# Second SwiGLU product: part loads a round ahead, residual tiles loaded singly, the final norm's halves on two engines

## The chip, the cores and the metric

One core of a Trainium2 chip runs the whole program. The metric is the device time of one launch in microseconds. The program before was timed three times.

## The reference, cut to what matters

The program is one layer of a streaming encoder on 1024 tokens of width 1024, in float32. After three token mixers and an output projection with a residual, which give `x`, comes the part that is changed:

```python
h = rms_norm(x, norm_ffn_g[l])
gate, up = jnp.split(h @ w_ffn_in[l], 2, axis=-1)
x = x + (jax.nn.silu(gate) * up) @ w_ffn_out[l]
...
return rms_norm(x, final_norm_g)   # x * rsqrt(mean(x*x) + 1e-6) * g
```

The hidden width of the SwiGLU is 2816, which is 22 tiles of 128, or 11 pairs of tiles ("j").

## The kernel before, in words

Every float32 product is made of three float32r matmuls (lines 132 to 134) on operands split into a high part (cast on ACT, line 125) and a low part (subtraction on DVE, line 126). The large products follow a Strassen-like scheme: a block product is seven products (p = 0 to 6) of sums of quarters instead of eight. The sums of the left side are made on DVE (line 901).

The class `Blocks` runs such products over units n. `make` prepares the left operand of the next product, up to seven products ahead. `product` issues the matmuls of (n, p). `after` empties or adds what they gave. For each n the sums "a" and "b" stand in one PSUM tile of two banks, and "c" in a third bank, begun by a copy of "a" on ACT (line 958).

The gate and up products are `fb`, over 22 units. Each finished quarter of silu(gate) times up is written to the DRAM tensor `m_d` by line 1231, from tiles of the pool `fb`. Meanwhile `right_units` splits the weights of the second product and parks them in the DRAM tensor `wt_d`.

The second product is `f2`, of class `Second`, over 16 rounds. A round (t, j0, j1) takes token tiles t and t + 4 and the pairs j0 to j1 of the hidden width; rounds 0 and 1 take two pairs, so 6 matmuls for a product, and later ones two or three pairs. Its left side is read back from `m_d` in two halves (i = 0, 1) by line 1318, inside `mid_sums`: one half in the two buffers "wr", which the weights of `fb` use before, the other in two buffers "mr" of the pool `fc`; round 0 has both halves in "wr". Its right side are tiles `tt` in a ring of 14, read from `wt_d` by line 1296; tiles 12 and 13 of the ring lie in `fc`. Each product of a round is added to the residual tile `x3` at line 1334; `load_x3(t)` (lines 1298 to 1302) brings tokens t and t + 4 as two transfers into one tile of the pool `keep`. Tiles wait for each other as wholes: a product into "a" waits until the addition that reads "b" of the same round is done.

The pool `fc` is opened at line 1382, after `fb` is released, and takes the same memory.

In the last round of a token tile `final(t, half)` makes the norm: ACT squares a half with a sum (line 1398), a small DVE operation follows (line 1400), and with the second half come another small DVE operation (1403), a power of -0.5 on POOL (1404) and on DVE two products of x, the root and the gain `fng` (1406), each with a DMA to the output (1407).

All DMAs here are issued by SP, which takes them in order. The order on every engine comes from a planner that simulates the program: of the instructions that are ready in its simulation it takes the one that stands first in the program, so that instructions can be moved ahead of blocked ones. On the chip each engine then keeps that order.

Of the kernel before, what the change touches and what calls it, by code (L numbers as in the profile page):

```python
# [7 lines left out]
F32 = mybir.dt.float32  # L8
F32R = mybir.dt.float32r
U8 = mybir.dt.uint8  # L10
AF = mybir.ActivationFunctionType
ALU = mybir.AluOpType
# [4 lines left out]
P = 128  # L17
S = 1024
D = 1024
# [9 lines left out]
EPS = 1e-6  # L29
# [42 lines left out]
def body(nc, tc, I, out):  # L72
    x_d, w_d, wf_d, wfup_d, par_d, lq_d, cst_d, msk_d, ffg_d, fng_d = I
    vec, act, pe, pool, sp = nc.vector, nc.scalar, nc.tensor, nc.gpsimd, nc.sync
# [3 lines left out]
    wp = tc.alloc_tile_pool(name="wp", bufs=2)  # L78
# [6 lines left out]
    y2 = lambda name: yp.tile([P, HALF], F32, tag="y2", name=name)  # L85
    s2 = lambda name: sp4.tile([P, HALF], F32, tag="s2", name=name, bufs=4)
# [5 lines left out]
    sm = cpool.tile([P, 32], F32, name="sm")  # L92
# [25 lines left out]
    def f(ap):  # L118
        return ap.bitcast(F32)
# [30 lines left out]
    def like(ap, src):  # L150
        if len(src.shape) == 2:
            return ap
        return ap[:, 0:src.shape[1] * src.shape[2]].rearrange("p (k n) -> p k n", k=src.shape[1])
# [6 lines left out]
    def operand(src, pin=False):  # L160
        if not spare:
            th, tl = wtiles()
            spare.extend((th[:, i, :], tl[:, i, :]) for i in range(2))
        wh, wl = spare.popleft()
        hilo(like(wh, src), like(wl, src), src, pin)
        return wh, wl
# [71 lines left out]
    def spawn(gen, after=0):  # L238
        clock["seq"] += 1
        heapq.heappush(events, (clock["now"] + after, clock["seq"], gen))  # L240
# [47 lines left out]
    def drain():  # L288
        while events:
            clock["now"] = max(clock["now"], events[0][0])  # L290
            resume()
# [47 lines left out]
    def hs(half):  # L339
        return slice(half * HALF, (half + 1) * HALF)  # L340
# [81 lines left out]
    for j in range(2):  # L422
        vec.tensor_tensor(out=lt[:, j * 64:(j + 1) * 64], in0=lq[:, j * 128:j * 128 + 64],
                          in1=lq[:, j * 128 + 64:j * 128 + 128], op=ALU.mult)
# [470 lines left out]
    def lefts(alloc, a11, a21, a12, a22):  # L895
        s_ = {0: a11, 3: a12, 5: a22}
        p = None

        def comb(to, a, b, op):
            s_[to] = like(alloc("s"), a11)  # L900
            vec.tensor_tensor(out=s_[to], in0=a, in1=b, op=op)

        while True:
            p = yield operand(s_[p]) if p is not None else None
            if p == 1:
                comb(1, a21, a22, ALU.add)
            elif p == 2:
                comb(2, s_[1], a11, ALU.subtract)
            elif p == 4:
                comb(4, a11, a21, ALU.subtract)  # L910
            elif p == 6:
                comb(6, a12, s_[2], ALU.subtract)

    def of(blocks):
        return lambda n, p: [tuple(b[:, k, :] for b in blocks[right[p]]) for k in range(4)]
# [105 lines left out]
    order = [(0, 0), (0, 3), (0, 1), (0, 2), (0, 4)]  # L1021
# [185 lines left out]
    order = [(0, 0), (0, 3), (1, 0), (1, 3), (0, 1), (1, 1), (0, 2), (1, 2), (0, 4), (1, 4), (0, 6), (1, 6), (0, 5)]  # L1207
# [34 lines left out]
    def t4_block():  # L1242
        for k in range(4):
            u, v = c2("u"), c2("v")
            for o, p in ((u, 0), (v, 1)):
                vec.tensor_tensor(out=o, in0=f(B["21"][p][:, k, :]), in1=f(B["T2"][p][:, k, :]), op=ALU.subtract)
            vec.tensor_tensor(out=u, in0=u, in1=v, op=ALU.add)
            hilo(B["T4"][0][:, k, :], B["T4"][1][:, k, :], u)
            yield 3
# [37 lines left out]
    tt, x3 = {}, {}  # L1287

    def load_t(i):
        if i >= NTL:  # L1290
            return
        at = i % RING
        pool_, tag = (keep, "kb") if at in (0, 1, 6, 7) else (big, "big") if at < 12 else (fcs["fc"], "tt")
        tt[i] = pool_.tile([P, 4, HALF], F32R, tag=tag, name="tt", bufs=8 if at < 12 else 2)
        n = 2 if i == NTL - 1 and 7 * PAIRS % 2 else 4
        sp.dma_start(f(tt[i][:, 0:n, :]), wt_d[i][:, 0:n, :])

    def load_x3(t):
        x = keep.tile([P, 2, D], F32, tag="kb", name="x3")
        for i in range(2):  # L1300
            sp.dma_start(x[:, i, :], x2_d[t + 4 * i])
            x3[t + 4 * i] = x[:, i, :]


    ROUNDS = [(0, 0, 2), (1, 0, 2), (2, 0, 3), (3, 0, 3), (0, 2, 4), (1, 2, 5), (2, 3, 6), (3, 3, 6),
              (0, 4, 7), (1, 5, 8), (2, 6, 9), (3, 6, 9), (0, 7, 11), (1, 8, 11), (2, 9, 11), (3, 9, 11)]
    fcs = {}

    def mid_sums(n):
        t, j0, j1 = ROUNDS[n]  # L1310
        v = []
        for i in range(2):
            if i and n:
                raw = fcs["fc"].tile([P, 1024], F32, tag="mr", name="mr", bufs=2)
            else:
                raw = wp.tile([P, 1024], F32, tag="wr", name="wr", bufs=2)
            raw = raw[:, 0:(j1 - j0) * 2 * P].rearrange("p (j b c) -> p j b c", j=j1 - j0, b=2)
            sp.dma_start(raw, m_d[j0:j1, t, :, 2 * i:2 * i + 2, :].rearrange("j p b c -> p j b c"))
            v += [raw[:, :, b, :] for b in range(2)]
        return lefts(s2, *v)  # L1320

    def unit_of(j, p):
        u = 7 * j + p
# [25 lines left out]
    for i, at in last_use.items():  # L1349
        loads.setdefault(at, []).append(i + RING)  # L1350
    f2 = Second(order2, makes2, mid_sums, lambda n, p: [unit_of(j, p) for j in range(*ROUNDS[n][1:])],
                None, None, 0)

    fb = Blocks(order, makes, ffn_sums, of(B), finish, copy, 6)
    for _ in range(4):
        fb.make()
    for at, (n, p) in enumerate(order):
        if at == 4:
            drain()
            tail.release()  # L1360
            fbs.append(tc.alloc_tile_pool(name="fb", bufs=1))
            spawn(t4_block(), 7)
        for _ in range(2 if at > 4 else 1):
            if len(fb.made) < (4 if at < 12 else AHEAD):
                fb.make()
        fb.product(n, p)
        if at == 14:
            spawn(right_units(), 0)
        if n == NU - 1:
            for i in {0: (2, 3), 1: (4, 5), 2: (6, 7), 3: (8, 9), 6: (10, 11)}.get(p, ()):  # L1370
                load_t(i)
            for t in {4: (0, 1), 5: (2, 3)}.get(p, ()):
                load_x3(t)
        if fb.nxt == len(order) and f2.nxt < 7 and len(fb.made) + len(f2.made) < AHEAD:
            f2.make()
        fb.after(n, p)
# [4 lines left out]

    fc = tc.alloc_tile_pool(name="fc", bufs=1)
    fcs["fc"] = fc
    for i in (12, 13):
        load_t(i)
    fng = fc.tile([P, D], F32, tag="fng", name="fng")
    sp.dma_start(fng, fng_d)
    norm = {}

    def final(t, half):  # L1390

        if t not in norm:
            norm[t] = fc.tile([P, D], F32, tag="xn", name="xn", bufs=2)
            a, other = sm[:, t:t + 1], None
        else:
            a, other = sm[:, 8 + t:9 + t], sm[:, t:t + 1]
        xn = norm[t]
        act.activation(xn[:, hs(half)], x3[t][:, hs(half)], AF.Square, accum_out=a)
        if other is None:
            vec.tensor_scalar(out=a, in0=a, scalar1=D * EPS, scalar2=None, op0=ALU.add)  # L1400
            return
        rc = sm[:, 16 + t:17 + t]
        vec.tensor_scalar(out=rc, in0=a, scalar1=other, scalar2=1.0 / D, op0=ALU.add, op1=ALU.mult)
        pool.tensor_tensor(out=rc, in0=rc, in1=mhalf[:, 0:1], op=ALU.pow)
        for c in (hs(0), hs(1)):
            vec.scalar_tensor_tensor(out=xn[:, c], in0=x3[t][:, c], scalar=rc, in1=fng[:, c], op0=ALU.mult, op1=ALU.mult)
            sp.dma_start(out[t, :, c], xn[:, c])

    for at, (n, p) in enumerate(order2):
        for _ in range(2):  # L1410
            if len(f2.made) < AHEAD:
                f2.make()
        f2.product(n, p)
        f2.after(n, p)
        for i in loads.get(at, ()):
            load_t(i)
# [59 lines left out]
def _program(arrays):  # L1476
    import concourse.bacc as bacc

    nc = bacc.Bacc("TRN2", target_bir_lowering=False, num_devices=1, dynamic_dma_scratch_size=1024)
    ins = [nc.dram_tensor(n, v.shape, mybir.dt.from_np(v.dtype), kind="ExternalInput").ap() for n, v in arrays.items()]  # L1480
    out = nc.dram_tensor("out_0_dram", (NT, P, D), F32, kind="ExternalOutput").ap()
    with tile.TileContext(nc) as tc:
        body(nc, tc, ins, out)
    return nc
# [9 lines left out]
```

## Time and profile before

| | us |
|---|---|
| median of 3 runs | 2070.02 (2068.46 to 2072.39) |
| profiled execution, its own time | 2069.95 |
| its span in the profile | 2068.2 |
| PE busy | 2013.6 (97%) |
| DVE busy | 1466.8 (71%) |
| ACT busy | 924.8 (45%) |
| POOL busy | 56.7 (3%) |

The span is what the trace covers; 1.75 us of the execution's own time lie around it. "Idle before" in a row is the time in which the engine stood, and the arrow names what ended it. PEclk is the granted clock of the matmul engine as a share of its full 2.4 GHz; half of it, 1.2 GHz, is its other level. Sizes are in units of 128 partitions by elements.

### The profile page before, as it was taken

To read this page: it belongs to the slowest core of one execution; us is meant where nothing else is said; L and a number is where in the kernel's file an instruction comes from. 1 tells how busy PE (TensorE), PEld (TensorE's weight loads), DVE (VectorE), ACT (ScalarE), POOL (GpSimd) and SP (SyncE) were. 2 spreads that over 40 slices of the span, in tenths; PEclk is the share of its full clock that TensorE was granted. 3 is DMA by queue.
4 is the path that set the end of the run, shared out by engine and by line. 5 is a ranking of instruction groups with operands and counts; after the bars stand their busy time and mean duration, and the time that the engine had idled before them with its cause. 6 is when DMAs were issued, how large, how long until landed. Compare 5 with 4: busy or idle time off the path is not lost.

```text
span 2068.2 us, 27247 instructions
## 1 busy us (share of the span) xinstructions
PE 2013.6 (97%) x10280; PEld 1694.9 (82%) x10280; DVE 1466.8 (71%) x2314; ACT 924.8 (45%) x1960; POOL 56.7 (3%) x64
## 2 busy tenths in 40 slices
PE   7999999999999999999999999999999999969997
PEld 6888878799999888898988888878888878847775
DVE  7997878677667787877874475469776776446566
ACT  6434433445534455555555452235444445312223
POOL 1000000000000000000000000000000000000000
PEclk9999999999999999999999999999999999989999
DMA  4232243312324444425243644414676666776652
GB/s 157 97 127 88 82 130 104 117 47 67 98 73 116 134 112 100 97 65 133 68 108 108 227 162 140 137 67 140 227 250 223 234 236 230 254 289 237 229 184 87
DMA packets 125124, 298.75 MB, mean 144 GB/s; under 512 B 11744, under 2 KB 56416, under 8 KB 115264
## 3 DMA queue, kind: packets, MB, share of 16 engines
q1 hardware_dynamic: 122256, 290.19, 42.1%
q0 software_dynamic: 2736, 6.82, 2.1%
q8 instruction: 81, 1.33, 0.3%
q14 instruction: 51, 0.42, 0.1%
HBM read 183.19 MB, written 94.90 MB: 134 GB/s over the span
## 4 chain that ended last, share of the span: by engine, by line
PE 68%; issue 13%; DVE 9%; DMA 6%; ACT 3%; POOL 1%; SPq 0%; DVEq 0%; POOLq 0%; ACTq 0%
PE sc L132 11%; PE sc L133 11%; PE sc L134 11%; PE pb L132 11%; PE pb L133 11%; PE pb L134 10%; DVE acc L448 1%; DMA wr<-w_dram 1%; DMA m_d<-t 1%; DMA wo<-w_dram 1%; DVE wl L126 1%; DMA wt_d<-to 1%; PE pb L766 1%; ACT p L739 1%; POOL rs L139 1%
## 5 line engine op out<-in xcount | busy, mean ns | idle before, releaser
L448 DVE SCALAR_TENSOR_TENSOR acc<-up,par,acc 128x1024 f32<-128x1024 f32 x240 | 306.2, 1276 | 0.6
L132 PE MATMUL pb<-h,wh 128*128 128x512 f32 x704 | 281.0, 399 | 1.0 <-ACT hf L310 1.0
L134 PE MATMUL pb<-h,wl 128*128 128x512 f32 x704 | 275.5, 391 | 0.0
L133 PE MATMUL pb<-h,wh 128*128 128x512 f32 x704 | 275.3, 391 | 0.0
L125 ACT CAST wh<-wr 128x512 fp32r<-128x512 f32 (+2 forms) x265 | 157.2, 611 | 187.7 <-PE pb L133 68.6
L126 DVE TENSOR_TENSOR wl<-wr,wh 128x512 fp32r<-128x512 f32 (+2 forms) x265 | 176.2, 673 | 75.4 <-ACT wh L125 73.7
L125 ACT CAST wh<-s 128x512 fp32r<-128x512 f32 (+2 forms) x216 | 123.6, 580 | 216.7 <-PE sc L133 137.9
L134 PEld LDWEIGHTS pb<-h,wl 128*128 128x128 f32 x704 | 132.3, 188 | 28.4
L132 PEld LDWEIGHTS pb<-h,wh 128*128 128x128 f32 x704 | 132.7, 188 | 26.0 <-ACT hf L310 1.2
L133 PEld LDWEIGHTS pb<-h,wh 128*128 128x128 f32 x704 | 132.6, 188 | 23.6 <-issue 0.2
L132 PE MATMUL pb<-wh,h 128*128 128x256 f32 x512 | 148.4, 290 | 0.0
L126 DVE TENSOR_TENSOR wl<-s,wh 128x512 fp32r<-128x512 f32 (+2 forms) x216 | 134.8, 635 | 17.8 <-ACT wh L125 17.8
L134 PE MATMUL pb<-wh,h 128*128 128x256 f32 x512 | 144.8, 283 | 0.0
L133 PE MATMUL pb<-wl,h 128*128 128x256 f32 x512 | 144.7, 283 | 0.0
L132 PE MATMUL sc<-bT,wh 128*128 128x512 f32 x352 | 137.4, 391 | 0.9 <-DVE t L1223 0.8
L133 PE MATMUL sc<-bT,wh 128*128 128x512 f32 x352 | 137.0, 389 | 0.0
L134 PE MATMUL sc<-bT,wl 128*128 128x512 f32 x352 | 137.0, 389 | 0.0
L132 PE MATMUL sc<-tt,wh 128*128 128x512 f32 x264 | 107.7, 413 | 22.4 <-ACT wh L125 15.3
L133 PE MATMUL sc<-tt,wh 128*128 128x512 f32 x264 | 104.6, 396 | 0.0
L134 PE MATMUL sc<-tt,wl 128*128 128x512 f32 x264 | 104.1, 396 | 0.0
L1334 DVE TENSOR_TENSOR x<-x,sc 128x512 f32<-128x512 f32 x80 | 54.5, 685 | 67.8 <-PE sc L134 66.5
L132 PE MATMUL sc<-T,wh 128*128 128x512 f32 x256 | 100.0, 391 | 1.9 <-ACT c L986 1.4
(300 smaller groups left out, 4567.5 us busy)
## 6 DMA issues: line engine op xcount, KB each, us to landing
wr<-w_dram SPq DMA_DIRECT2D x146, 512.0 KB, 3.7
wt_d<-to SPq DMA_DIRECT2D x38, 1024.0 KB, 4.2
tt<-wt_d SPq DMA_DIRECT2D x38, 1024.0 KB, 5.6
m_d<-t SPq DMA_DIRECT2D x44, 256.0 KB, 4.2
wo<-w_dram SPq DMA_DIRECT2D x22, 512.0 KB, 5.8
k<-k SPq DMA_DIRECT2D x48, 128.0 KB, 2.6
kl<-kl SPq DMA_DIRECT2D x48, 128.0 KB, 2.4
xt<-x_dram SPq DMA_DIRECT2D x8, 512.0 KB, 8.1
```

The source lines that it names most:

```text
L125: a = act.copy(hi, src)
L126: b = vec.tensor_tensor(out=lo, in0=src, in1=f(hi), op=ALU.subtract)
L132: pe.matmul(o, ah, bh, start=start, stop=False, skip_group_check=more)
L133: pe.matmul(o, ah, bl, start=False, stop=False, skip_group_check=more)
L134: pe.matmul(o, al, bh, start=False, stop=stop, skip_group_check=more)
L139: pool.tensor_tensor(out=dst, in0=dst, in1=mhalf[:, 0:width], op=ALU.pow)
L448: op = vec.scalar_tensor_tensor(out=acc, in0=up[:, j:j + S], scalar=w, in1=acc, op0=ALU.mult, op1=ALU.add)
L739: act.activation((p0[:, 0:n], p1)[i], sc[i], AF.Exp, bias=st_[:, i:i + 1], accum_out=st_[:, 2 + i:3 + i])
L766: pe.matmul(ov[:, 0:P], parts[k // 4][:, c], a["v"][:, k, :], start=k == 0, stop=k == nk - 1)
L1334: vec.tensor_tensor(out=x, in0=x, in1=ch["bacaab"[p - 1]], op=ALU.add)
```

## The change: what it does

Part loads: `mid_sums` loads nothing of its own round any more. A new function `load_mid(n)` loads both halves of round n: round 0 into two small buffers "mr0" (tag "y2"), odd rounds into both "wr" buffers, even rounds from 2 on into both "mr" buffers of `fc`. Round 0 is asked for twelve products before the end of `fb`, round 1 once all left operands of `fb` are made, round 2 as the first thing in `fc`, and round n + 1 by `mid_sums(n)`.

Residual tiles: before, `load_x3(0)` to `load_x3(3)` (four times two transfers) stood in the last unit of `fb`. Now only `load_x3(0)` stands there, `load_x3(1)` after the opening of `fc` and the loads of round 2, and 2 and 3 with the first products of rounds 1 and 2. Ring tiles 12 and 13 and the gain `fng` move from the opening of `fc` to the first products of rounds 2 and 4.

Final norm: with the first half DVE now multiplies x by the gain; with the second half ACT scales that product by the root while DVE makes the other half as before. The gain is multiplied by 32 once, on ACT, so that the mean's division by 1024 falls away.

```diff
-    def mid_sums(n):
+    mid = {}
+
+    def load_mid(n):
+        if n >= len(ROUNDS) or n in mid:
+            return
         t, j0, j1 = ROUNDS[n]
-        v = []
+        mid[n] = []
         for i in range(2):
-            if i and n:
+            if n == 0:
+                raw = y2("mr0")
+            elif n % 2:
+                raw = wp.tile([P, 1024], F32, tag="wr", name="wr", bufs=2)
+            else:
                 raw = fcs["fc"].tile([P, 1024], F32, tag="mr", name="mr", bufs=2)
-            else:
-                raw = wp.tile([P, 1024], F32, tag="wr", name="wr", bufs=2)
...
+    def mid_sums(n):
+        if n:
+            load_mid(n + 1)
+        return lefts(s2, *mid[n])
...
-            for t in {4: (0, 1), 5: (2, 3)}.get(p, ()):
-                load_x3(t)
+            if p == 4:
+                load_x3(0)
+        if at == len(order) - 12:
+            load_mid(0)
+        if fb.nxt == len(order):
+            load_mid(1)
...
-    for i in (12, 13):
-        load_t(i)
+    load_mid(2)
+    load_x3(1)
     fng = fc.tile([P, D], F32, tag="fng", name="fng")
-    sp.dma_start(fng, fng_d)
...
+            act.activation(xn[:, c], x3[t][:, c], AF.Square, accum_out=sm[:, t:t + 1])
+            vec.tensor_tensor(out=xn[:, c], in0=x3[t][:, c], in1=fng[:, c], op=ALU.mult)
             return
...
+        vec.tensor_scalar(out=rc, in0=a, scalar1=sm[:, t:t + 1], scalar2=D * EPS, op0=ALU.add, op1=ALU.add)
         pool.tensor_tensor(out=rc, in0=rc, in1=mhalf[:, 0:1], op=ALU.pow)
-        for c in (hs(0), hs(1)):
-            vec.scalar_tensor_tensor(out=xn[:, c], in0=x3[t][:, c], scalar=rc, in1=fng[:, c], op0=ALU.mult, op1=ALU.mult)
-            sp.dma_start(out[t, :, c], xn[:, c])
+        o = hs(1 - half)
+        act.activation(xn[:, o], xn[:, o], AF.Copy, scale=rc)
+        vec.scalar_tensor_tensor(out=xn[:, c], in0=x3[t][:, c], scalar=rc, in1=fng[:, c], op0=ALU.mult, op1=ALU.mult)
+        for q in (o, c):
+            sp.dma_start(out[t, :, q], xn[:, q])
...
+        if p == 0 and n in (1, 2):
+            load_x3(n + 1)
+        if (n, p) == (2, 0):
+            for i in (12, 13):
+                load_t(i)
+        if (n, p) == (4, 0):
+            sp.dma_start(fng, fng_d)
+            act.activation(fng, fng, AF.Copy, scale=ROOT)
```

## Rows read from the trace of the kernel before

**Rows 1.** The page, part 1: busy time, share of the span, instructions.
```profile
PE 2013.6 (97%) x10280; PEld 1694.9 (82%) x10280; DVE 1466.8 (71%) x2314; ACT 924.8 (45%) x1960; POOL 56.7 (3%) x64
```

**Rows 2.** Windows: stretch, length; busy (instructions) by engine; PEclk, DMA share, GB/s.
```profile
1740.00:1780.00 40.00, 40.00 (x177) 32.76 (x176) 26.73 (x43) 17.18 (x31) 0.00 (x0) 1.00 0.73 251
1815.00:1850.00 35.00, 17.31 (x54) 11.97 (x55) 11.44 (x25) 4.35 (x11) 0.00 (x0) 0.76 0.91 341
1850.00:2020.00 170.00, 169.21 (x721) 132.85 (x720) 107.66 (x202) 45.27 (x96) 0.00 (x0) 1.00 0.57 203
2020.00:2053.00 33.00, 31.54 (x133) 23.97 (x131) 24.75 (x55) 13.31 (x36) 2.98 (x5) 1.00 0.20 73
2053.00:2068.20 15.20, 4.53 (x12) 2.89 (x12) 7.68 (x16) 3.61 (x10) 1.65 (x3) 0.77 0.36 138
```

**Rows 3.** Timeline of PE: start us, us, instruction, idle before and releaser.
```profile
1822.84 0.50 PE L132 MATMUL sc<-tt,wh 128*128 128x512 f32 x1 [0.78 <-DVE x L1334]
...
1825.29 0.50 PE L132 MATMUL sc<-tt,wh 128*128 128x512 f32 x1 [0.78 <-DVE x L1334]
...
1835.87 0.80 PE L132 MATMUL sc<-tt,wh 128*128 128x512 f32 x1 [8.93 <-ACT wh L125]
...
2054.54 0.77 PE L132 MATMUL sc<-tt,wh 128*128 128x512 f32 x1 [2.26 <-ACT xn L1398]
...
2058.22 0.50 PE L132 MATMUL sc<-tt,wh 128*128 128x512 f32 x1 [0.78 <-DVE sm L1400]
```

**Rows 4.** Waits from 1800 to 1850 us (ACT, then SP): total, times, longest.
```profile
ACT wh L125 <- DMA wr<-m_d: 20.0, 1, 20.0
...
SPq L1296 <- DMA m_d<-t: 8.4, 2, 5.6
```

**Rows 5.** Timeline of DVE: the last gate-and-up tile.
```profile
1815.57 0.69 DVE L1230 TENSOR_TENSOR t<-t 128x512 f32<-128x512 f32 x1
```

**Rows 6.** Timeline of SP: the DMAs it issues around the change of products.
```profile
1810.25 0.37 SPq L1231 DMA_DIRECT2D m_d<-t  x1
1811.51 4.93 SPq L1301 DMA_DIRECT2D x<-x_d  x4
1816.54 1.77 SPq L1231 DMA_DIRECT2D m_d<-t  x1
1818.86 2.77 SPq L1296 DMA_DIRECT2D tt<-wt_d  x2
1822.06 0.37 SPq L1231 DMA_DIRECT2D m_d<-t  x1
...
1834.75 0.81 SPq L1296 DMA_DIRECT2D tt<-wt_d  x2
```

**Rows 7.** DMAs issued near 1810.3, 1822.1 and 1836 us: KB, us to landing.
```profile
m_d<-t SPq DMA_DIRECT2D x1, 256.0 KB, 11.8
...
m_d<-t SPq DMA_DIRECT2D x1, 256.0 KB, 12.7
...
fng<-fng_dram SPq DMA_DIRECT2D x1, 512.0 KB, 7.8
mr<-m_d SPq DMA_DIRECT2D x1, 256.0 KB, 8.0
```

**Rows 8.** Timeline of DVE, and of ACT (one row), at the end.
```profile
2051.78 1.42 DVE L1406 SCALAR_TENSOR_TENSOR xn<-x,sm,fng 128x512 f32<-128x512 f32 x2 [0.66 <-POOL sm L1404]
2053.11 1.28 DVE L1334 TENSOR_TENSOR x<-x,sc 128x512 f32<-128x512 f32 x2
...
2059.83 1.42 DVE L1406 SCALAR_TENSOR_TENSOR xn<-x,sm,fng 128x512 f32<-128x512 f32 x2 [0.66 <-POOL sm L1404]
2061.16 0.68 DVE L1334 TENSOR_TENSOR x<-x,sc 128x512 f32<-128x512 f32 x1
...
2061.88 0.63 ACT L1398 ACTIVATE xn<-x 128x512 f32<-128x512 f32 x1 [2.14 <-DVE x L1334]
...
2063.51 1.41 DVE L1406 SCALAR_TENSOR_TENSOR xn<-x,sm,fng 128x512 f32<-128x512 f32 x2 [0.67 <-POOL sm L1404]
```

More of the change, by code (lines that the diff above doesn't have):

```diff
@@ L1307, in body @@
     fcs = {}
-    def mid_sums(n):
+    mid = {}
+    def load_mid(n):
+        if n >= len(ROUNDS) or n in mid:
+            return
         t, j0, j1 = ROUNDS[n]
-        v = []
+        mid[n] = []
         for i in range(2):
-            if i and n:
+            if n == 0:
[3 more added lines that the diff above has]
+            else:
                 raw = fcs["fc"].tile([P, 1024], F32, tag="mr", name="mr", bufs=2)
-            else:
-                raw = wp.tile([P, 1024], F32, tag="wr", name="wr", bufs=2)
             raw = raw[:, 0:(j1 - j0) * 2 * P].rearrange("p (j b c) -> p j b c", j=j1 - j0, b=2)
             sp.dma_start(raw, m_d[j0:j1, t, :, 2 * i:2 * i + 2, :].rearrange("j p b c -> p j b c"))
-            v += [raw[:, :, b, :] for b in range(2)]
-        return lefts(s2, *v)
+            mid[n] += [raw[:, :, b, :] for b in range(2)]
+    def mid_sums(n):
+        if n:
+            load_mid(n + 1)
+        return lefts(s2, *mid[n])
     def unit_of(j, p):
@@ L1383, in body @@
     fcs["fc"] = fc
-    for i in (12, 13):
-        load_t(i)
+    load_mid(2)
+    load_x3(1)
     fng = fc.tile([P, D], F32, tag="fng", name="fng")
-    sp.dma_start(fng, fng_d)
+    ROOT = 32.0
+    assert ROOT * ROOT == D
     norm = {}
     def final(t, half):
+        c = hs(half)
         if t not in norm:
[L1393 to L1400, printed above, removed]
+            xn = norm[t] = fc.tile([P, D], F32, tag="xn", name="xn", bufs=2)
+            act.activation(xn[:, c], x3[t][:, c], AF.Square, accum_out=sm[:, t:t + 1])
+            vec.tensor_tensor(out=xn[:, c], in0=x3[t][:, c], in1=fng[:, c], op=ALU.mult)
             return
-        rc = sm[:, 16 + t:17 + t]
-        vec.tensor_scalar(out=rc, in0=a, scalar1=other, scalar2=1.0 / D, op0=ALU.add, op1=ALU.mult)
+        xn, a, rc = norm[t], sm[:, 8 + t:9 + t], sm[:, 16 + t:17 + t]
+        act.activation(xn[:, c], x3[t][:, c], AF.Square, accum_out=a)
+        vec.tensor_scalar(out=rc, in0=a, scalar1=sm[:, t:t + 1], scalar2=D * EPS, op0=ALU.add, op1=ALU.add)
         pool.tensor_tensor(out=rc, in0=rc, in1=mhalf[:, 0:1], op=ALU.pow)
-        for c in (hs(0), hs(1)):
-            vec.scalar_tensor_tensor(out=xn[:, c], in0=x3[t][:, c], scalar=rc, in1=fng[:, c], op0=ALU.mult, op1=ALU.mult)
-            sp.dma_start(out[t, :, c], xn[:, c])
+        o = hs(1 - half)
[3 more added lines that the diff above has]
+            sp.dma_start(out[t, :, q], xn[:, q])
     for at, (n, p) in enumerate(order2):
```

## The prediction

> **What bounds the kernel now.** I read the page's first part, then windows over the last 700 us, then PE's timeline, the waits and SP's timeline in the one stretch where PE stands. PE is busy 97% of the span [rows 1], so whatever PE does not wait for is worth nothing. At full pace it issues 177 matmuls in 40 us, 0.226 us each [rows 2]. That rate turns each window into lost time, since matmul records on the page overlap:
>
> - 1815 to 1850: 54 matmuls are 12.2 us of work in 35 us, so 22.8 us are lost. The granted clock is 0.76 there, a mix of 2.4 and 1.2 GHz.
> - 1850 to 2020: 721 matmuls are 162.9 us, 7.1 us lost in 170, in many small gaps.
> - 2020 to 2053: 133 are 30.1 us, 2.9 lost.
> - 2053 to the end: 12 are 2.7 us in 15.2, so 12.5 us of tail, the clock at 0.77.
>
> The first stretch is the change of products. PE does round 0 alone, where each product stands 0.78 us for the addition of the one before, and then stands 8.93 us [rows 3]. ACT has stood 20.0 us there for a part load of round 1 [rows 4]. The second half of round 1 comes later still, issued at about 1836 and 8.0 us on its way [rows 7].
>
> Why these loads are late is in SP's order [rows 6, 7]. The gate-and-up write of 1810.25 lands 11.8 us later, at 1822.05; the last such write is issued at 1822.06. Between the two SP issues four residual transfers, one write and two ring tiles, so the last write is the eighth behind. I read this as eight transfers in flight and no more: SP stands until the eighth before has landed. The tile of that last write was ready at 1815.57 + 0.69 = 1816.3 [rows 5], so 5.8 us go there. It lands at 1822.06 + 12.7 = 1834.8, and ring tile 12, the first thing in the new pool, is issued at 1834.75: the new pool opens with that landing, although tile 12 itself waits for no data of it. SP's wait at line 1296 for this write is in [rows 4].
>
> Transfers land in the order of issue and at one rate: between the two landings, 12.7 us, went four halves of residual tiles (2.1 MB), two ring tiles (2.1 MB) and two writes (0.5 MB), 4.7 MB or 0.37 MB/us.
>
> **The change part by part.** All sums are against the profiled execution, 2069.95 us (span 2068.2 and 1.75 around it), which is 0.07 us from the median of the three runs.
>
> *Rounds 0 and 1.* No transfer is added: 32 part loads before and after, of the same bytes. Round 0 moves to buffers free long before, and round 1 takes the two "wr" buffers that round 0 had, so both halves land before 1810 where round 0's did in time. PE then has 14 products of 6 matmuls, 14 x 1.36 = 19.0 us of work, from about 1813. That removes the 8.93 us wait and the one after it.
>
> *What is late next, the residual tile of round 1.* SP no longer issues the six transfers of `load_x3(1)` to `(3)` ahead of the last write. The write of 1810.25 had `load_x3(1)` in front (1.05 MB, 2.8 us), so it lands at 1819.2. Behind it stand one write, two ring tiles and the last write, 2.6 MB or 7.1 us: the last write lands at 1826.3 instead of 1834.8. Then comes `load_x3(1)`, which the planner can put in front of the blocked loads of round 2: 1829.1. Without it PE can do round 0, and of round 1 products 0, 1 and 3: ten products, 13.6 us, plus some 1.5 us at the start where round 0 has no partner, to 1828.2. With the addition (0.69) PE goes on at 1829.9, a stand of 1.7 us.
>
> *Round 2's parts* (0.79 MB, 2.1 us) are issued when the new pool opens, 1826.3. They land at about 1831 if only `load_x3(1)` is in front. If the planner has also moved `load_x3(2)` and `(3)` ahead (2.1 MB, 5.7 us) it is 1837. The four products of round 1 left then run alone and pay the 0.78 us gap and a slow first matmul each (spacing 2.45 in [rows 3] against 1.36, so 1.1): one to three times, 1.1 to 3.3 us.
>
> So the hole costs 1.5 + 1.7 + 1.1 to 3.3, 4.3 to 6.5 us, and if the stand lowers the clock another 1.3 (an estimate: six matmuls at 1.2 GHz instead of 2.4 lose about 0.21 each; behind the 2.26 us stand [rows 3] the clock is 0.77 over the window [rows 2]). A stand of 0.78 did not lower it; 1.7 lies between. I take 6.5 in all: the hole gives back 22.8 - 6.5 = 16.3 us. Bounds: 1.5 lost (21.3 back) if everything is in time, and nothing back.
>
> *Residual tiles 2 and 3, ring tiles 12 and 13* come later than now, but PE uses them 6 to 45 us after the hole; the queue is at 57% from 1850 on [rows 2]. Cost 0. If that cover is gone, each 1.05 MB in front of a needed one costs 2.8 us.
>
> *The gain on ACT.* One ACT operation over twice the width of a square's 0.63 us [rows 8], so at most 1.3 us on an engine that is busy 45 of 170 us [rows 2]. But it waits for the gain's transfer, 7.8 us in flight today [rows 7], and ACT takes its work in order: the casts behind it (made up to seven products ahead, 7 x 2.0 us at 9 matmuls each) and the copy that begins "c", which has one product, 2.0 us, of cover. From 0 to 7.8 - 2.0 = 5.8; 0.3 taken, since the planner puts the operation where its own simulation has the data.
>
> *The end.* DVE loses eight of the sixteen products of 0.71 (a pair takes 1.42 [rows 8]) and gets eight plain ones, for which the addition's 0.68 is the nearest row. Three places count. (a) The last product but one waits 2.26 us, because the addition at 2053.11 stands behind the pair of 2051.78: one product fewer is -0.7, a new one in the same queue up to +0.7; I take -0.2. If the stand then stays short enough for the clock, six matmuls give 1.3 back; I take -0.4. (b) The last addition, at 2061.16, stands behind the pair of 2059.83: -0.7. (c) The last pair of 2063.51 becomes one DVE product beside one ACT scaling of about 0.63: -0.7. ACT's scaling waits for POOL behind the square, some 0.9 us in which ACT's casts stand, but ACT is busy 3.6 of the last 15.2 us; +0.2. The end gives 1.8, between +0.5 lost and 3.4 gained.
>
> Sum: -16.3 - 1.8 + 0.3 = -17.8, so 2069.95 - 17.8 = 2052.2 us. From the median it is 2052.2 too.
>
> *A rule weighed.* The two writes landed after everything issued before them, 11.8 and 12.7 us for 256 KB [rows 7], and the sum takes this order. The Trainium skill ("DMA: Bandwidth & Descriptors", section "Queues, rings and completion order") says that completion is not first-in first-out per issuing engine, that a later transfer may finish before an earlier one. By it the last write could land some 3 us after its issue at 1816.5, and the hole would shrink to the first rival below; the trace speaks for order.
>
> **The rivals.**
>
> 1. *Everything in time*, about 2045.5: the last write and round 1's residual tile land before PE runs out, 1.5 us stay of the hole and the end gives all: -21.3 - 3.4 + 0.3. For it: ten products of cover. Against it: 3.9 MB behind the write of 1810.25 at 0.37 MB/us.
> 2. *The residual tile behind round 2's parts on SP*, about 2058: those wait for the last write (1826.3), land at about 1830.5, and `load_x3(1)` at 1833.3; PE goes on at 1834 after 5.8 us, or after 10 if DVE stands in order at round 1's first addition (1824) with round 0's last two behind it; then 6 to 10 matmuls at 1.2 GHz, 1.3 to 2.1. Lost 10.4 to 14.7, mean 12.5: 22.8 - 12.5 + 1.8 - 0.3 = 11.8 back. For it: program order. Against it: the planner takes what is ready in its simulation ahead of what is blocked.
> 3. *It does not do what it says*: round 1's parts are still late, since the "wr" buffers come free late or SP holds the loads behind ring tiles. Only the end gains: 2068. Against it: round 0's halves had the same buffers and were not waited for.
> 4. *Slower*, about 2072: ACT stands at the scaling of the gain. The transfer is issued in SP's line behind ring tiles that wait for PE, and lands more than 20 us after ACT has reached the operation; then the stand less 2.0 of cover outweighs the 18 won. At 12.7 in flight plus the 8.4 that SP has stood at line 1296 [rows 4], and 1.3 for the clock, it is 20.4 lost. It decides from 20 us on; below 8 it does not show.
>
> **How the numbers follow.** Forecast 0.54 (2049 to 2056), rival 1 0.16, rival 2 0.20, rival 3 0.06, rival 4 0.04. No change means within 0.2%, 4.1 us, about what a measurement of this kernel can tell: rival 3 lies there. So faster 0.90, same 0.06, slower 0.04. The range reaches over most of rivals 1 and 2, 2046 to 2061; rivals 3 and 4 and their like stay out.
>
> **What would show it.** In the trace after, PE's first wait on an ACT cast at about 1827 is gone, and 1815 to 1850 has some 120 matmuls or more instead of 54. The last gate-and-up write lands at about 1826, and the loads of round 2 are issued at that moment. The largest stand in the hole is under 4 us and ends with line 1334's addition, for rival 2 over 5. From the last matmul to the span's end go 1.3 us less. ACT's wait for the gain is under 3 us. The forecast is wrong if round 2's parts, not round 1's residual tile, end the longest stand with over 8 us, or if the end grows.

## The result, and the profile after

The changed kernel takes 2049.0 us (median of 4 runs, 2047.8 to 2051.0) against 2070.2 of the kernel before in the same session: ratio 0.9897, 95% interval 0.9885 to 0.9909. Forecast were 2052.2 us in a range of 2046 to 2061. The profiled execution has 2049.43 us and a span of 2047.7, so the span is 20.5 us shorter than the 2068.2 us before.

The page's first part: PE does the same 10280 matmuls, DVE has eight operations fewer, ACT nine more.

```profile
## 1 busy us (share of the span) xinstructions
PE 2009.8 (98%) x10280; PEld 1693.7 (83%) x10280; DVE 1466.8 (72%) x2306; ACT 930.4 (45%) x1969; POOL 56.6 (3%) x64
```

The windows that answer to [rows 2], in its columns:

```profile
1815.00:1850.00 35.00, 33.05 (x134) 25.73 (x135) 24.07 (x49) 10.63 (x23) 0.00 (x0) 0.95 0.92 346
1850.00:2020.00 170.00, 167.93 (x716) 131.53 (x715) 108.15 (x203) 47.96 (x106) 1.21 (x2) 1.00 0.58 205
2020.00:2053.00 33.00, 17.46 (x71) 12.42 (x70) 17.08 (x33) 13.16 (x33) 3.40 (x6) 0.93 0.25 96
```

From 1815 to 1850 there are 134 matmuls instead of 54; at 0.226 us each 4.7 us are lost there and not 22.8. SP's timeline in the same stretch, which answers to [rows 6] (start, duration of the issue, line, destination and source):

```profile
1813.89 1.35 SPq L1296 DMA_DIRECT2D tt<-wt_d  x2
1815.78 0.37 SPq L1231 DMA_DIRECT2D m_d<-t  x1
1816.20 1.72 SPq L1301 DMA_DIRECT2D x<-x_d  x2
1826.69 0.90 SPq L1324 DMA_DIRECT2D mr<-m_d  x2
```

The last gate-and-up write leaves at 1815.78 instead of 1822.06, residual tile 1 right behind it, and the loads of round 2 stand until 1826.69, when the write has landed and the new pool opens. It took 10.9 us from the write's issue to the loads that wait for it, in order behind what was asked before. The section that the prediction weighed (the Trainium skill, "DMA: Bandwidth & Descriptors", section "Queues, rings and completion order") says that completion is not first-in first-out per issuing engine; no overtaking shows here. That section names no time to landing: the "some 3 us" that the prediction put beside it are its own, and no run here shows a landing that early.

PE's timeline, first the two places where it stands around the change of products, then the one in mid-section and the last two (start, duration, line, tiles; in brackets the stand and what ended it):

```profile
1814.96 0.47 PE L132 MATMUL sc<-tt,wh 128*128 128x512 f32 x1 [0.42 <-DVE t L1223]
1829.83 0.50 PE L132 MATMUL sc<-tt,wh 128*128 128x512 f32 x1 [1.95 <-DVE x L1344]
...
1917.59 0.47 PE L132 MATMUL sc<-tt,wh 128*128 128x512 f32 x1 [1.74 <-DVE x L1344]
...
2035.97 0.47 PE L132 MATMUL sc<-tt,wh 128*128 128x512 f32 x1 [1.29 <-DVE x L1344]
...
2038.38 0.50 PE L132 MATMUL sc<-tt,wh 128*128 128x512 f32 x1 [0.78 <-DVE x L1344]
```

The 8.93 us stand of [rows 3] is gone. What is left, 1.95 us, ends with an addition of DVE, and DVE's timeline says what that waited for:

```profile
1829.09 0.69 DVE L1344 TENSOR_TENSOR x<-x,sc 128x512 f32<-128x512 f32 x1 [0.33 <-DMA x<-x_d]
```

It is the landing of the second half of residual tile 1. Line 1344 is the addition that was line 1334.

### The profile page after: what moved, and what is told of

Read it like the earlier page. It is cut to its first block, busy times and chain, and to the rows that moved or that the text cites. A ratio compares the mean times of both kernels' runs of the same rounds, so it can differ in the third digit from the quotient of the medians.

```text
span 2047.7 us, 27244 instructions
## 1 busy us (share of the span) xinstructions
PE 2009.8 (98%) x10280; PEld 1693.7 (83%) x10280; DVE 1466.8 (72%) x2306; ACT 930.4 (45%) x1969; POOL 56.6 (3%) x64
## 4 chain that ended last, share of the span: by engine, by line
PE 72%; issue 13%; DVE 7%; DMA 4%; ACT 3%; POOL 1%; SPq 0%; POOLq 0%; ACTq 0%; DVEq 0%
PE sc L132 12%; PE sc L133 12%; PE sc L134 12%; PE pb L132 11%; PE pb L133 11%; PE pb L134 11%; DVE acc L448 1%; DMA wo<-w_dram 1%; PE pb L766 1%; ACT p L739 1%; DMA wr<-w_dram 1%; DMA wt_d<-to 1%; POOL rs L139 1%; DMA x<-x_d 1%; PE sc L729 1%
## 5 line engine op out<-in xcount | busy, mean ns | idle before, releaser
L126 DVE TENSOR_TENSOR wl<-s,wh 128x512 fp32r<-128x512 f32 (+2 forms) x216 | 135.4, 638 | 16.4 <-ACT wh L125 16.3
```

The lines of the kernel that those rows point to most:

```text
L126: b = vec.tensor_tensor(out=lo, in0=src, in1=f(hi), op=ALU.subtract)
```

## The experiments

Ratios are to the kernel before, run on the same chip in the same session, with 95% intervals.

**Each part alone.** The first three are the kernel before with one part of the change, the fourth is the changed kernel without the new norm. The part loads alone ("the parts"), as a difference to that fourth kernel; residual tiles, ring tiles 12 and 13 and the gain go back to their old places:

```diff
-            if p == 4:
-                load_x3(0)
+            for t in {4: (0, 1), 5: (2, 3)}.get(p, ()):
+                load_x3(t)
...
     load_mid(2)
-    load_x3(1)
+    for i in (12, 13):
+        load_t(i)
     fng = fc.tile([P, D], F32, tag="fng", name="fng")
+    sp.dma_start(fng, fng_d)
...
-        if p == 0 and n in (1, 2):
-            load_x3(n + 1)
-        if (n, p) == (2, 0):
-            for i in (12, 13):
-                load_t(i)
-        if (n, p) == (4, 0):
-            sp.dma_start(fng, fng_d)
```

> The kernel before with one part of the change: the part loads asked a round ahead into the buffers of the change. Residual tiles, ring tiles 12 and 13, the gain and the final norm stay as before. Theory (the prediction's queue): the last gate-and-up write is again issued at about 1822 and lands at about 1834.8, because the same six residual transfers stand in front of it; x3(1) is there early, so PE runs rounds 0 and 1 without a stand (14 products, 19 us, to about 1833) and then stands for round 2's parts, which are issued when the new pool opens at about 1835 and land at about 1839 or 1840. Lost from 1815 to 1850: 1.5 at the start, some 7 to 8 of stand, some 2 of low clock, about 11 us instead of 22.8. Time about 2059 (2056 to 2062). Rival A (the parts alone make the gain, the residual tiles are hidden anyway): 2051 to 2052, the after kernel's time without its end. Rival B (the parts gain nothing while the tiles stand in front of the last write): 2068 to 2070.

Measured: 2056.2 us, ratio 0.9935 (0.9923 to 0.9948), 13.5 us less. The window, the write's issue, the issue of round 2's loads and PE's longest stand, from three views of its trace:

```profile
1815.00:1850.00 35.00, 28.77 (x119) 21.00 (x118) 22.00 (x43) 9.22 (x21) 0.00 (x0) 1.00 0.92 352
```
```profile
1824.06 0.37 SPq L1231 DMA_DIRECT2D m_d<-t  x1
1825.29 3.83 SPq L1324 DMA_DIRECT2D wr<-m_d  x2
1835.40 0.89 SPq L1324 DMA_DIRECT2D mr<-m_d  x2
```
```profile
1839.59 0.50 PE L132 MATMUL sc<-tt,wh 128*128 128x512 f32 x1 [2.43 <-ACT wh L125]
```

The queue is as expected (1824 and 1835.4), the stand is not: 2.43 us where I had 7 to 8. PE reached the end of round 1 only at 1837 and not at 1833, because its last products already ran alone (two stands of 0.87 us in the same timeline), and the parts were there at 1839. A second stand of 1.63 us follows at 1843.71. Lost 35 - 119 x 0.226 = 8.1 us instead of 11.

The tiles alone (edit: the kernel before with the change's four places of `load_x3`, `load_t(12)`, `load_t(13)` and of the gain's load):

> The kernel before with another part of the change: residual tiles 1 to 3 and ring tiles 12 and 13 one by one where the change puts them, the gain's transfer with round 4. The part loads stay as before (second half of round 1 in the new pool, asked when its sums are made), and so does the final norm. Theory: the last gate-and-up write is issued when its tile is ready, at about 1816, and lands at about 1826 instead of 1834.8; round 1's late half follows at once and lands at about 1831 (behind residual tile 1), so PE goes on at about 1832.5 instead of 1844: 8 to 10 us gained, time about 2061 (2059 to 2064). Rival A: round 1's other half waits for the buffers of round 0 and PE still stands as long, under 3 us gained, 2067 to 2070. Rival B: the tiles alone give nearly all, 2053 or less.

Measured: 2059.7 us, 0.9952 (0.9939 to 0.9964), 9.9 us less, the time that the theory had. The half that ends PE's stand of 4.02 us is not the one that it named, though. ACT's cast there waits for round 1's first half ("wr"), asked at 1819.65 and landed 11.7 us later. From PE's and ACT's timeline, with matmuls 0.43 us apart behind the stand:

```profile
1831.87 0.80 PE L132 MATMUL sc<-tt,wh 128*128 128x512 f32 x1 [4.02 <-ACT wh L125]
1832.46 0.63 PE L133 MATMUL sc<-tt,wh 128*128 128x512 f32 x1
1832.89 0.63 PE L134 MATMUL sc<-tt,wl 128*128 128x512 f32 x1
```
```profile
1831.41 0.40 ACT L125 CAST wh<-wr 128x256 fp32r<-128x256 f32 x1 [15.07 <-DMA wr<-m_d]
```

The late half ("mr") is asked at 1828.20 and lands 3.9 us later, so the second stand that the kernel before has in its hole is gone:

```profile
1845.20 0.80 PE L132 MATMUL sc<-tt,wh 128*128 128x512 f32 x1 [6.41 <-ACT wh L125]
```

Before, that half was issued behind ring tiles 12 and 13 and the gain, 2.6 MB [rows 6, 7], and took 8.0 us. So part of the 9.9 us can come from those three out of its way and not from the residual tiles; the run does not separate the two.

The new norm alone, and the change without it (edit: `final` and the gain's scaling exchanged; the first of the two also moves the gain's transfer to round 4):

> The kernel before with the new final norm alone (gain scaled on ACT, plain product with the gain for the first half, the two halves of the last step on ACT and DVE side by side, the gain's transfer with round 4); part loads, residual and ring tiles as before. Theory of the prediction: 1.8 us less, time about 2068.4; the stand of 2.26 us before the last product but one is shorter, and from the last matmul to the end 1.3 us go. Rival (what the trace of the changed kernel suggests): only 0.4 us go behind the last matmul, and what was won between 1850 and the last matmul comes from elsewhere, so 2069.8, no change that can be told.

> The changed kernel with the old final norm (both halves of a tile scaled by DVE pairs at the end; the gain not scaled), all else of the change kept. Theory of the prediction: 1.8 us more than the changed kernel, about 2050.8, with the stand of about 2.3 us before the last product but one and the slow matmuls behind it back. Rival 1: 0.4 us more, 2049.4. Rival 2 (all that was won between 1850 and the end comes from the new norm): 2.6 us more, 2051.6.

Measured: the norm alone 2068.3 us, 0.9990 (0.9981 to 0.9999), 2.1 us less; the change without it 2051.5 us, 0.9915 (0.9901 to 0.9928), 17.6 us less than before and some 3.6 more than the changed kernel, with intervals that still touch. So the norm is worth 2 to 3.6 us by these times. Some of the 2.1 can be the gain's transfer, which in that run no longer stands in front of round 1's late half: the second stand is 5.16 us there instead of 6.41. Parts and tiles alone gave 13.5 + 9.9 = 23.4, together 17.6: 5.8 us of the same 22.8 lost in the hole are won by either.

PE's timeline shows what the norm does. Its stand before the last product but one, first in the norm alone, then in the change without the norm, with the next two matmuls:

```profile
2054.49 0.47 PE L132 MATMUL sc<-tt,wh 128*128 128x512 f32 x1 [1.25 <-ACT xn L1399]
```
```profile
2035.04 0.69 PE L132 MATMUL sc<-tt,wh 128*128 128x512 f32 x1 [2.25 <-DVE x L1344]
2035.52 0.63 PE L133 MATMUL sc<-tt,wh 128*128 128x512 f32 x1
2035.95 0.63 PE L134 MATMUL sc<-tt,wl 128*128 128x512 f32 x1
```

With the new norm it is 1.25 and 1.29 us, without it 2.25 and 2.26 [rows 3], and in these two without it the six matmuls behind it are 0.43 us apart instead of 0.23. The stand belongs to the old norm, the slow matmuls do not always: with the tiles alone (2.23 us) and in the run with pairs of transfers below (2.25 us), both with the old norm, they are 0.23 us apart, and the next stand is 1.36 us instead of 0.78. PE's timeline of the run with pairs:

```profile
2055.48 0.47 PE L132 MATMUL sc<-tt,wh 128*128 128x512 f32 x1 [2.25 <-ACT xn L1398]
2058.47 0.50 PE L132 MATMUL sc<-tt,wh 128*128 128x512 f32 x1 [1.36 <-DVE sm L1400]
```

From the matmul ahead of that stand to the span's end the five traces with the old norm take 15.3 to 16.3 us and the nine with the new one 13.3 to 13.8.

**The stand that is left.** Four edits of the changed kernel move residual tile 1 or round 2's parts.

```diff
-            for i in {0: (2, 3), 1: (4, 5), 2: (6, 7), 3: (8, 9), 6: (10, 11)}.get(p, ()):
+            for i in {0: (2, 3), 1: (4, 5), 2: (6, 7), 3: (8, 9)}.get(p, ()):
                 load_t(i)
-            if p == 4:
-                load_x3(0)
+            for t in {4: (0,), 5: (1,)}.get(p, ()):
+                load_x3(t)
...
     load_mid(2)
-    load_x3(1)
+    for i in (10, 11):
+        load_t(i)
```

> The changed kernel with residual tile 1 asked one product earlier, in front of the last two gate-and-up writes, and ring tiles 10 and 11 (2.1 MB) behind the part loads of round 2 instead of in front of the last write. Theory: the stand of 1.95 us that ends with round 1's first addition goes, and with it the nine matmuls at 1.2 GHz behind it (1.9 us); 1.05 MB more and 2.1 MB less stand in front of the last write, so it lands some 2.8 us earlier, near 1824, and round 2's parts are there by about 1829, before PE asks for them; ring tiles 10 and 11 are first used with round 2's last unit, later than they land. 2.5 to 4 us faster than the changed kernel: 2045 to 2046.5. Rival A: round 2's parts or ring tile 10 become the late ones, PE stands as long, 2048.5 to 2050. Rival B: the stand is not the tile's but the order of additions on DVE; no change, 2049.

```diff
     load_mid(2)
+    load_x3(2)
     load_x3(1)
...
-        if p == 0 and n in (1, 2):
-            load_x3(n + 1)
+        if p == 0 and n == 2:
+            load_x3(3)
```

> The changed kernel with residual tile 2 asked in front of round 2's part loads and residual tile 1 behind them (they change places; this is the order of the prediction's second rival). Theory: PE's stand in the change of products ends with the landing of residual tile 1, so it ends as much later as that lands: issued at about 1827.7 instead of 1816.2, behind 0.79 MB, landing at about 1833 to 1834 instead of 1829; the stand grows from 1.95 to about 6 or 7 us, part of round 1's work moves behind it. 4 to 6 us slower than the changed kernel, 2053 to 2055. Rival A: another thing (the parts of round 2, the casts) ends the stand, so it hardly grows: 2049 to 2050. Rival B (as that rival was priced, with DVE standing in order): 2057 to 2059.

Measured: tile ahead 2050.7 us, 0.9903 (0.9888 to 0.9918); tile behind 2050.3 us, 0.9903 (0.9888 to 0.9917). Neither can be told from the changed kernel, and both theories fell. With the tile ahead the pool opens at 1822.89, near the 1824 expected, and round 2's first cast runs at 1826.45. But DVE takes round 2 up only at 1832.39, behind four additions of round 1, and PE, which then runs these products alone, stands 0.93, 0.78 and 0.87 us. From ACT's, DVE's and PE's timeline of that run:

```profile
1826.45 0.51 ACT L125 CAST wh<-mr 128x384 fp32r<-128x384 f32 x1 [2.03 <-PE sc L134]
```
```profile
1831.79 0.69 DVE L1344 TENSOR_TENSOR x<-x,sc 128x512 f32<-128x512 f32 x1 [1.75 <-PE sc L134]
1832.39 0.55 DVE L126 TENSOR_TENSOR wl<-mr,wh 128x384 fp32r<-128x384 f32 x1
```
```profile
1827.65 0.50 PE L132 MATMUL sc<-tt,wh 128*128 128x512 f32 x1 [0.93 <-DVE x L1344]
1830.09 0.50 PE L132 MATMUL sc<-tt,wh 128*128 128x512 f32 x1 [0.78 <-DVE x L1344]
1832.62 0.47 PE L132 MATMUL sc<-tt,wh 128*128 128x512 f32 x1 [0.87 <-DVE x L1344]
```

With the tile behind, the planner changed DVE's and PE's order as well: round 1's first additions went behind round 2's sums, and the stand, 2.55 us, ends with a cast of round 2's parts instead. From PE's and DVE's timeline:

```profile
1832.30 0.56 PE L132 MATMUL sc<-tt,wh 128*128 128x512 f32 x1 [2.55 <-ACT wh L125]
```

```profile
1834.56 0.55 DVE L901 TENSOR_TENSOR s<-mr 128x384 f32<-128x384 f32 x1
1835.03 0.55 DVE L126 TENSOR_TENSOR wl<-s,wh 128x384 fp32r<-128x384 f32 x1
1835.49 0.68 DVE L1344 TENSOR_TENSOR x<-x,pb 128x512 f32<-128x512 f32 x1
```

So I also brought round 2's parts forward, into a buffer that waits for no pool, first alone and then with the tile ahead:

```diff
+        if n == 2:
+            both = keep.tile([P, 2, D], F32, tag="kb", name="mr2")
...
+            elif n == 2:
+                raw = both[:, i, :]
...
             load_mid(1)
+            load_mid(2)
```

> The changed kernel itself, beside the next two, for a direct comparison. 2048 to 2050.5; if the spread between rounds is all there is between it and the runs with a tile or the gain moved (ratios 0.9888 to 0.9903 so far), its ratio lies among theirs.

> The changed kernel with round 2's part loads in a buffer of the pool of residual tiles, asked with round 1's, so that they wait neither for the last gate-and-up write nor for the new pool; residual tile 1 stays behind the last write. Theory: in the changed kernel the stand of 1.95 us could not be filled because round 2's sums were not there; now PE can do round 2's products while residual tile 1 is under way, the stand and the nine slow matmuls go, 2 to 4 us: 2045 to 2047. 0.79 MB more stand in front of the last write and so of residual tile 1 (2.1 us later, about 1831). Rival: the later residual tiles 1 and 2 take back what is won, 2048 to 2051.

> As the run before, and with residual tile 1 one product earlier and ring tiles 10 and 11 behind (as in the run with the tile ahead). Theory: in that run the stand of the tile was gone but round 1's last four products ran alone, because DVE took round 2's sums up only behind round 1's additions; with round 2's parts there early the order is mixed, no product runs alone, and PE stands nowhere over 0.5 us from 1815 to 1850: 150 to 155 matmuls there instead of 134. 3 to 5 us faster than the changed kernel, 2044 to 2046. Rival: ring tiles 10 and 11 or residual tile 2, pushed back, become the late ones; 2048 to 2051.

Measured: the changed kernel again 2048.5 us, 0.9898 (0.9884 to 0.9913); round 2 early 2051.0 us, 0.9912 (0.9897 to 0.9927); both early 2049.7 us, 0.9908 (0.9892 to 0.9925). No gain. Round 2 early is even slower than the changed kernel beside it, by about 2.5 us: all four of its runs (2050.55 to 2052.07) lie above all four (2047.58 to 2048.92); its rival had 2048 to 2051. Both early lies in its rival's range. The windows of the three, in this order:

```profile
1815.00:1850.00 35.00, 32.39 (x137) 24.84 (x137) 24.46 (x48) 10.49 (x22) 0.00 (x0) 1.00 0.91 344
```
```profile
1815.00:1850.00 35.00, 31.39 (x128) 22.73 (x128) 22.96 (x45) 8.94 (x20) 0.00 (x0) 1.00 0.85 323
```
```profile
1815.00:1850.00 35.00, 32.01 (x133) 24.36 (x134) 23.41 (x47) 9.92 (x22) 0.00 (x0) 1.00 0.86 331
```

The long stand is gone in both, but smaller ones take its place: 0.51, 0.87, 0.66, 0.79 and 0.78 us with round 2 early, 0.51, 0.87 and 1.38 with both. I found no version that beats the changed kernel.

**Bytes or number of transfers.** The kernel before with pairs of residual transfers made one:

```diff
-        for i in range(2):
-            sp.dma_start(x[:, i, :], x2_d[t + 4 * i])
+        sp.dma_start(x, x2_d[t:t + 5:4].rearrange("i p d -> p i d"))
```

> The kernel before with each pair of residual transfers made one of twice the size: the same bytes in the same order, four transfers less in front of the last gate-and-up write. Theory (what delays that write is the bytes queued ahead of it): SP comes to it earlier, but it lands at the same time, about 1834 to 1835, the pool opens with it, and the time is that of before, 2069 to 2071. Rival (the prediction's 5.8 us that go because SP stands until the eighth transfer before has landed are lost in themselves): the write is issued at about 1816 to 1818 and lands 4 to 6 us earlier, at about 1829 to 1831, time 2064 to 2066.

Measured: 2070.9 us, 1.0004 (0.9994 to 1.0013), and the pool opens at 1835.23 as before:

```profile
1821.37 1.13 SPq L1231 DMA_DIRECT2D m_d<-t  x1
1822.59 3.92 SPq L1318 DMA_DIRECT2D wr<-m_d  x2
1835.23 0.81 SPq L1296 DMA_DIRECT2D tt<-wt_d  x2
```

Four transfers fewer with the same bytes change nothing in the landing. But SP still came to the write only at 1821.37. The count of eight did not hold it there: the eighth transfer before, a ring tile issued at 1808.23, had landed 11.0 us later, at 1819.2. SP stood at a ring tile that waited for PE, as the list of SP's waits from 1815 to 1824 has it:

```profile
SPq L1296 <- PE pb L134: 2.4, 1, 2.4
```

So the run takes the count away as the reason for the late landing, and does not show what the write would do if SP came to it early with the same bytes ahead; that is open.

**The gain and the tail.**

```diff
     assert ROOT * ROOT == D
+    sp.dma_start(fng, fng_d)
+    act.activation(fng, fng, AF.Copy, scale=ROOT)
...
-        if (n, p) == (4, 0):
-            sp.dma_start(fng, fng_d)
-            act.activation(fng, fng, AF.Copy, scale=ROOT)
```

> The changed kernel with the gain's transfer (0.5 MB) and its scaling on ACT taken up when the new pool opens, behind round 2's part loads, instead of with round 4 (the place that the prediction's rival 4 needs). Theory: ACT comes to the scaling at about 1832, stands until the transfer lands at about 1833 to 1835 and then takes 1.06 us, while PE still has products of round 1; residual tile 2 comes 1.4 us later, when it is not yet needed. Within 1.5 us of the changed kernel, 2049 to 2050.5. Rival: the casts behind the scaling are late, PE stands over 2 us and the clock falls: 2052 to 2056.

Measured: 2047.5 us, 0.9888 (0.9872 to 0.9905), not to be told from the changed kernel. ACT's scaling did not stand at all: the planner put it behind four casts of round 2, which had waited long enough themselves.

```profile
1834.33 1.05 ACT L1404 ACTIVATE fng<-fng 128x1024 f32<-128x1024 f32 x1
```

```diff
-        for q in (o, c):
-            sp.dma_start(out[t, :, q], xn[:, q])
+        act.dma_start(out[t, :, o], xn[:, o])
+        sp.dma_start(out[t, :, c], xn[:, c])
```

> The changed kernel with the two output transfers of a tile issued by two engines (ACT its half, SP the other), so that neither waits for the other's issue of about 0.4 us. What it tells is the tail, from the start of the last scaling on DVE to the span's end, 4.69 us both before and after the change. Theory (the 0.5 MB of both halves pass at one rate, 0.37 MB/us, 1.4 us from the first issue on, so the end hangs on when the first half is ready, 0.75 to 0.78 us after the scaling starts in either kernel): 4.6 to 4.8 us again. Rival (the second issue behind the first on SP is what took the gain): 4.2 to 4.4 us. Time 2048 to 2050 either way; a place where ACT's transfers stand before casts could add up to 1 us.

Measured: 2049.9 us, 0.9906 (0.9888 to 0.9923). The last scaling starts at 2043.00 in a span of 2047.8: 4.8 us, nothing gained, as the theory had it.

## Why the prediction was right

**The hole** was to give back 16.3 us. Its window gave 22.8 - 4.7 = 18.1. A window holds different matmuls of the two kernels, so I also counted back from the last matmul: the changed kernel starts the 920th from the end, ahead of the hole, 0.3 us earlier (1813.92 and 1814.20), and the 800th, behind it, 18.5 us earlier (1846.52 and 1865.03). So 18.2 came in the hole. Each step came where it was put: write issued 1815.8 (forecast about 1816.3) and landed 1826.7 (1826.3); round 2's loads issued at that moment; residual tile 1's second half there at 1829.09 (1829.1); PE on at 1829.83 (1829.9) after 1.95 us (1.7). The clock behind the stand, an estimate of 1.3, cost about 1.4 (nine matmuls in 3.64 us) in this execution and nothing in the second profile of the same kernel (2.22 us), 137 matmuls in the window instead of 134. That it fell here is chance. Two terms were too dear. One was round 1's last products alone, 1.1 to 3.3 us. Residual tiles 2 and 3 did not get in front of round 2's parts, which came in time behind slow matmuls; in the second profile one gap of 0.72 us was left. The other was the start, 1.5, which took 0.42.

**From 1850 to 2020** 1.1 us more are lost: 170 - 716 x 0.226 = 8.2 instead of 7.1. Counted back from the last matmul, the lead falls from 18.5 at the 800th to 17.6 at the 13th, by 0.9. The stand of 1.74 at 1917.59, 0.35 at that place before, is all of that and more. Its cause is open (below). It is not tied to one part of the change: the tiles alone have 2.17 us there, the parts alone 1.73, the change without the norm none.

**The end** was to give 1.8 us. The 13th matmul from the end, just ahead of the stand, and the last, before and then after:

```profile
2051.89 0.39 PE L134 MATMUL sc<-tt,wl 128*128 128x512 f32 x1
2059.46 0.39 PE L134 MATMUL sc<-tt,wl 128*128 128x512 f32 x1
```
```profile
2034.29 0.39 PE L134 MATMUL sc<-tt,wl 128*128 128x512 f32 x1
2039.65 0.40 PE L134 MATMUL sc<-tt,wl 128*128 128x512 f32 x1
```

The twelve take 7.57 us before and 5.36 after, so 2.2 us came there, where step (a) had 0.6. The term was undersized: the stand fell by 1.0 (2.26 to 1.29) and the clock's 1.2 us came whole, six matmuls 0.23 apart instead of 0.43. The 1.2 hangs on the clock having fallen in the trace of before; with the old norm and no fall there the twelve take 6.9 us (tiles alone, and before with pairs). Step (b), the last addition, was right: it starts at 2040.67, 1.02 us behind the start of the last matmul, where before it was 1.70 [rows 8]. Step (c), 0.7 for the last halves side by side, failed, so the last matmul to the span's end gave 0.7 us (8.73 to 8.02) and not the 1.3 that the prediction named as a sign. Starts of the last scaling on DVE and ACT:

```profile
2043.01 0.75 DVE L1419 SCALAR_TENSOR_TENSOR xn<-x,sm,fng 128x512 f32<-128x512 f32 x1 [0.66 <-POOL sm L1416]
```
```profile
2043.01 0.72 ACT L1418 ACTIVATE xn<-xn,sm 128x512 f32<-128x512 f32 x1 [0.91 <-POOL sm L1416]
```

From there to the span's end it is 4.69 us; before, from 2063.51 [rows 8] to 2068.2, it was 4.69 too. The step took the end to hang on when both halves are made. What it hangs on is the first half: the output's bytes start when that is ready, and pass at one rate. The GB/s line of the DMA view in 40 slices, of the changed kernel from 2043.0 to 2047.8 (0.12 us a slice) and of the kernel before from 2064.0 to 2068.3 (0.11):

```profile
GB/s 0 0 0 0 0 0 0 0 0 0 0 0 0 256 375 358 410 358 427 359 358 427 358 427 239 17 0 0 0 0 0 0 0 0 0 0 0 0 0 0
```
```profile
GB/s 0 0 0 0 0 0 0 0 0 0 191 362 419 362 381 324 457 362 362 381 438 343 362 134 0 0 0 0 0 0 0 0 0 0 0 0 0 0 0 0
```

Both run without a break for about 1.5 us, from 1.55 and 1.57 us after the start of the scaling. The second product of DVE had been hidden behind the first half's transfer. Two issuing engines did not shorten it. No run delays one half alone, so this is read from the views.

**The gain** was priced 0.3 and cost nothing that shows: ACT stood 0.3 us for it, and nobody waited for ACT.

Sum: 0.3 ahead of the hole, 18.2 in it, -0.9 in mid-section, 2.2 in (a), 0.7 in (b) and 0 in (c) are 20.5 us, as in the spans. The forecast of 17.8 missed 2.7 of it: 0.3 ahead of the hole, 1.9 in it, 1.6 in (a) and 0.5 set aside for ACT and the gain, less 0.7 in (c) and 0.9 in mid-section.

**The rivals.** Rival 1 (2045.5) lies below every median, 2047.5 to 2051.0, of the changed kernel and its variants with the new norm: bringing tile and parts in time only put other stands there. Rival 2's order was run and cost nothing that shows, since the planner moved other work with the tile; its price stood on DVE keeping the old order. Rival 3 is out: the parts alone give 13.5 us. Rival 4 is out in the changed kernel by ACT's stand of 0.3 us. The run with the gain first does not make its condition: there the transfer went out early too, and not behind ring tiles.

## What to carry to other kernels

When one transfer gates a stage, count the bytes asked for ahead of it in its queue: six transfers of 0.5 MB moved from in front of one write to behind it brought it forward by 8 us. Gains of two edits that shorten the same wait do not add (13.5 and 9.9 alone, 17.6 together), and where a planner orders the engines, a late tile can be paid by other work put in its place, so price it by the whole order and not by its landing. At the end of a program ask when the first byte of the output can leave: what is made while it is under way is hidden.

## What the hardware showed that I had not expected

The clock after a stand does not follow from the stand's length. The granted clock stayed at 2.4 GHz behind 1.74 us (changed kernel), 1.85 (two issuing engines), 1.90 (second profile of the changed kernel), 2.17 (tiles alone), 2.25 (before with pairs) and 2.43 (parts alone), and matmuls ran at 1.2 GHz for a while behind 1.80 and 2.25 (change without the norm), 1.95 (changed kernel), 2.26 (before), 2.55 (tile behind) and 4.02 (tiles alone). With the gain first, stand 1.85 us, six matmuls ran at full pace first and the slow ones came after; with the tile ahead, stand 2.31, it was four. Two profiles of one and the same kernel differ in this at the same place, so a forecast should carry such a term as a chance and not as a sum. What decides it stays open.

DVE stood at one place in mid-section for a reason that no view names ("issue"), 3.03 us in the changed kernel and 3.08 in its second profile, 3.60 with the tile ahead, 1.94 with the gain first, 1.36 with the tile behind, and 1.65 at the same point of the kernel before:

```profile
1912.70 0.55 DVE L901 TENSOR_TENSOR s<-mr,s 128x384 f32<-128x384 f32 x1
1916.29 0.56 DVE L901 TENSOR_TENSOR s<-wr 128x384 f32<-128x384 f32 x1 [3.03 <-issue]
```

PE paid 1.74 and 1.80, 2.31, 0.62 and 0 us for it, and 0.35 before. The run with two issuing engines and the one with pairs show no such stand. That alone moves the time by nearly 0.1% between kernels that differ elsewhere; its cause was not tested.
